# A state-space layer's front on Trainium2: B and x products in column halves around the context product, and TensorE's order tied per chunk

## The chip, the cores and the metric

The kernel runs on one core of a Trainium2 chip. The core has a matrix engine (TensorE, in the profile PE, its weight loads PEld), a vector engine (VectorE, DVE), an activation engine (ScalarE, ACT), a third elementwise engine (GpSimd, POOL) and a queue that issues transfers (SyncE, SP). Each engine takes its instructions in a fixed order and waits at an instruction until that one's inputs and outputs are free. Matrix products land in PSUM, which has eight banks of 512 fp32 columns for 128 partitions.

The metric is the device time of the whole program in microseconds, as the median of several runs.

## The reference

Two layers work on a latent stream of 1024 positions and a context of 256, both 1024 wide. Layer 0 is windowed attention, and the change does not touch it. Layer 1 is a bidirectional Mamba-2 (SSD) mixer. What matters of it:

```
z, xbc, dt_raw = split(h @ w_in)                       # for latent and context
xbc = silu(centred_depthwise_conv(xbc, conv_w, conv_b))  # 5 taps, zero padding
xs, bm, cm = split(xbc)                # 8 groups of 4 heads of 64; B and C of 128 per group
dt = softplus(dt_raw + dt_bias)        # two directions
# context: only its final states s_f and s_b are wanted
# latent, each direction, in chunks of 128 positions, starting from s_f or s_b:
states = einsum(bm, decay_to_end, xs * dt)             # per chunk
h_prev = scan of the states over the chunks
y_diag = einsum(cm @ bm.T, lmat, xs * dt)              # inside a chunk
y_off  = einsum(cm, h_prev, exp(a_cs))                 # from earlier chunks
u = (y_f + y_b + d_skip * xs) * silu(z)
out = (rms_normalize per group (u) * norm_w) @ w_out
```

Then a gated residual and a final normalisation follow.

## The kernel before

Every product of layer 1's front is made of three matmuls per tile of 128 rows: operands are split into a high and a low part (wh, wl for weights, uH, uL for the stream), and high x high, low x high and high x low are summed in PSUM. The stream lies transposed, as two latent tiles of 512 columns and one context tile of 256.

**The group's front** (`front`, line 1022 on). The layer works by the 8 groups. The front of a group makes four convolved tiles of 128 channels, in the order B (`bT`), the two halves of x (`cacc`, called x0 and x1 here) and C (`cT`), and then z. For B, x0 and x1 (`nat` in the code) there is also the context's product. In the program's order a tile is: context product (24 matmuls of 256 columns, line 1085, into the one-bank tile `psD`), then the latent product (48 matmuls of 512 columns, line 1095, into the two-bank tile `raw` of slot `pj2`; each pair works on columns 0 to 511 and 512 to 1023). Only the first tile of the first group makes its latent product in two halves, with the dt product (line 1105) between them. z is 2 x 2 x 4 x 12 matmuls of 256 columns (line 1129), again into `pj2`.

**After a product** come the taps (`taps`): ScalarE scales the middle tap into `acc` (line 1007) and VectorE adds four shifted ones (line 1011), all reading `raw`; then `silu`: a tanh on ScalarE that writes over `raw` (line 1018) and a product on VectorE (line 1019). B and x are also needed with positions on the partitions, so `natural` turns them: TensorE transposes `acc` back into `raw` (line 1058) and ScalarE copies the result out (line 1061). For the latent tiles this is done in two steps of four transposes and one copy each. The weights of the next tile are split by ScalarE (line 1034) and VectorE (line 1038).

**Who issues when.** `front` is a generator that yields after each matmul, with its cost (`N512`, `N256`). What follows a product is put on a queue, `post`: per 0.5 us of yielded cost one step is issued, credit that is not used is kept, and steps marked `LATE` (turnings and what depends on them) are issued 3 us of cost later. 

**The scan** runs beside it. In the main loop (line 1340 on) `slot` handles one chunk of group g while `fill` runs a share of the front of group g+1 (75.65 us of cost by the program's rates, so 9.46 per chunk; in the last group it is the output product, line 1527). A slot opens with `pcb` = B.T C (line 1247), then the products with the carried states (lines 1249 and 1250, tile `po`), the next state (line 1256) and four products with the decay matrix M (line 1281); VectorE multiplies M by `pcb` (line 1251) and scales `po` (line 1260). At the next slot the finished rows are transposed (line 1312) and stored. Between the fills `tick` advances `states`, the backward chain of group g+1: GpSimd weights x (line 1173) and decays the state (line 1178), TensorE multiplies into `psD` (line 1198), and VectorE adds (line 1210), eleven times, one after the other.

**What sets the order.** The listing above is the program's order. When the program is built, a planner with its own model of time goes through it and may put an instruction of an engine ahead of an earlier one that it takes to be waiting, where no dependence forbids it. Buffers of a name are used in rotation: `pj2` has 2, `psX` (all tiles of a slot) 3, `psD` 1, which is all eight banks. `tc.issue_after(x)` holds the instructions of a block that run on x's engine behind x in that engine's order; it adds no wait.

Of the kernel before, what the change touches and what calls it, by code (L numbers as in the profile page):

```python
# [9 lines left out]
F32 = mybir.dt.float32  # L10
# [7 lines left out]
P = 128  # L18
D = 1024
KT = D // P  # L20
LAT = 1024
CTX = 256
# [20 lines left out]
    pj=1, S=2, pt=2, pv=1,  # L43
# [18 lines left out]
LATE = 3.0  # L62
# [49 lines left out]
class Kernel:  # L112
# [908 lines left out]
    def front(self, g, st, post, first=None, dt=None):  # L1021

        nc, t, a = self.nc, self.t, self.a
# [27 lines left out]
            return lambda: weights(a["w_z"][g, q], 4, 256)  # L1051

        def natural(raw, acc, dst, o, n):
            steps = []

            def tr(lo, hi):
                for x in range(lo, hi):
                    nc.tensor.transpose(raw[:, x * P : (x + 1) * P], acc[:, x * P : (x + 1) * P], self.ident)

            def ev(d, lo, hi):  # L1060
                nc.scalar.copy(d[:, :, o : o + P], raw[:, lo * P : hi * P].rearrange("p (c n) -> p c n", n=P))  # L1061
# [14 lines left out]
        for n, (x, kind) in enumerate(tiles):  # L1076
            need(w)
            cur, w = w, (weights(a["w_dt"], KT, P) if g + n == 0 else loads[n + 1]())
            nat = {"bT": ("bn", 0), 0: ("xn", 0), 1: ("xn", P)}.get(kind)
            wh, wl = cur["h"], cur["l"]  # L1080
            if nat:
                raw = t(ps, [P, 512], F32, "psD")[:, :CTX]
                for k in range(KT):
                    for y, (l, r) in enumerate(((wh, uH), (wh, uL), (wl, uH))):
                        nc.tensor.matmul(raw, l[:, k, :], r[2][:, k, :], start=k + y == 0, stop=k == KT - 1 and y == 2)  # L1085
                        yield N256
                acc = t(pf, [P, CTX], F32, "cctx")
                post.extend(self.taps(x, raw, acc, 0, CTX, CTX) + self.silu(raw, acc) + natural(raw, acc, [(st[nat[0]][2], 0, 2)], nat[1], 2))
            raw = t(ps, [P, LAT], F32, "pj2")
            acc = t(pf, [P, LAT], F32, "cacc") if nat and kind != "bT" else t(p, [P, LAT], F32, kind)  # L1090
            for q in ((0,), (1,)) if g == 0 and n == 0 else ((0, 1),):
                for k in range(KT):
                    for y, (l, r) in enumerate(((wh, uH), (wh, uL), (wl, uH))):
                        for i in q:
                            nc.tensor.matmul(raw[:, 512 * i : 512 * i + 512], l[:, k, :], r[i][:, k, :], start=k + y == 0, stop=k == KT - 1 and y == 2)  # L1095
                            yield N512
                    if k == 3 and (q[0] == 0 or g + n == 0):
                        post.extend(w["steps"])
                if g + n == 0 and q[0] == 0:
                    need(w)  # L1100
                    dw, w = w, loads[1]()
                    draw = t(ps, [P, 512], F32, "psX")
                    for k in range(KT):
                        for y, (l, r) in enumerate(((dw["h"], uH), (dw["h"], uL), (dw["l"], uH))):
                            nc.tensor.matmul(draw, l[:, k, :], r[1][:, k, :], start=k + y == 0, stop=k == KT - 1 and y == 2)
# [13 lines left out]
        for i in range(2):  # L1119
            pj = t(ps, [P, 4, 256], F32, "pj2")  # L1120
            for q in range(2):
                ww = (w0, w)[q]
                need(ww)
                for c in range(4):
                    for k in range(4):
                        u, v = uH[i][:, 4 * q + k, c * P : (c + 1) * P], uL[i][:, 4 * q + k, c * P : (c + 1) * P]
                        for y, (l, r) in enumerate(((u, ww["h"]), (u, ww["l"]), (v, ww["h"]))):

                            nc.tensor.matmul(pj[:, c], l, r[:, k, :], start=c % 2 + q + k + y == 0, stop=c % 2 == 1 and q == 1 and k == 3 and y == 2)  # L1129
# [12 lines left out]

            post.extend([tanh, prod])

    def ssd(self, c0):
# [92 lines left out]
        def slot(n, st, fill, tick):  # L1238
# [8 lines left out]
            nc.tensor.matmul(pcb, st["bT"][:, cs], st["cT"][:, cs], start=True, stop=True)  # L1247
            po = t(ps, [P, 512], F32, "psX")
            nc.tensor.matmul(po[:, :256], st["cT"][:, cs], flat(st["hf"]), start=True, stop=True)  # L1249
            nc.tensor.matmul(po[:, 256:], st["cT"][:, cs], flat(st["hb"][c]), start=True, stop=True)  # L1250
# [95 lines left out]
        with ExitStack():  # L1346
            for g in range(G):
# [41 lines left out]
    def ssd_out(self, p, spare, sp, sc, post):  # L1389
# [107 lines left out]
        for n, (i, mg, qs) in enumerate(sweeps):  # L1497
# [8 lines left out]
            for q in qs:  # L1506
# [5 lines left out]
                for z in range(2):  # L1512
# [11 lines left out]
                    for x in range(4):  # L1524
                        sl = slice(x * P, (x + 1) * P)
                        for y, (l, r) in enumerate(((w["h"], hi), (w["h"], lo), (w["l"], hi))):
                            nc.tensor.matmul(banks[x], l[:, z, sl], r, start=k == 2 * qs[0] and y == 0, stop=k == 2 * qs[-1] + 1 and y == 2)  # L1527
# [166 lines left out]
```

## Time and profile before

| | |
|---|---|
| time, median of 3 runs | 1811.74 us (1805.05 to 1812.2) |
| the profiled execution's own time | 1807.02 us |
| its span, first to last instruction | 1805.3 us |
| mean granted TensorE clock | 0.993 |
| first front of the SSD layer | about 747 to 849 us |
| seven groups, front of the next beside the scan | about 849 to 1591 us |
| last group's scan beside the output product | about 1591 to 1694 us |
| rest of the output product | to 1805 us |

How to read the rows that follow. A row of the page's first part has an engine's busy time, its share of the span and the number of instructions. A row of groups has the line, the engine, the operation and its tiles (written by the names of the program, buffer numbers left out; the slot `pj2` appears as pj), shapes and count, then busy time, the mean of one in ns, and after the second bar the idle time of the engine just before these instructions with what ended it. A row of a timeline has start, duration, engine, line, operation and count, and in brackets the idle time before it with its releaser. TensorE's durations overlap, since matmuls are pipelined: what a matmul costs is the distance from its start to the next one's. A row of stretches has the length, then busy time and count for PE, PEld, DVE, ACT and POOL, the granted clock, the DMA share and GB/s. A row of waits has who waited for whom, the total, how often, and the longest.

### The profile page before, as it was taken

What the parts mean: (1) busy time and instruction counts of PE and PEld (TensorE: products, weight loads), DVE (VectorE), ACT (ScalarE), POOL (GpSimd) and SP (SyncE); (2) the same over time, 40 slices, a digit from 0 to 9 for tenths busy, and PEclk for the clock granted to TensorE, in tenths of its full rate; (3) what the DMA queues carried; (4) which work ended last, traced back from release to release, by engine and by line L of the source; (5) the groups of instructions that cost most, each with busy time, mean ns of one, the idle gap of its engine ahead of it and who ended that gap; (6) DMA issues with size and microseconds to landing.
All of it is one profiled execution on the core that took longest, in us unless ns stands there. A gap on an engine that the chain in (4) does not pass through costs nothing.

```text
span 1805.3 us, 28983 instructions
## 1 busy us (share of the span) xinstructions
PE 1739.6 (96%) x10319; PEld 1494.7 (83%) x10319; DVE 1181.8 (65%) x2115; ACT 867.1 (48%) x1906; POOL 799.0 (44%) x1068
## 2 busy tenths in 40 slices
PE   6899999999999999999999999999999999999997
PEld 2697788888888887778888898988889898888887
DVE  4634436778877885684776858577684867766734
ACT  3612237777777774452443525344353534544522
POOL 2331127555575545103454544645454464554411
PEclk9999999999999999999999999999999999999999
DMA  9558856444455436222222323222332322656533
GB/s 334 226 144 268 283 177 149 106 100 111 111 153 130 120 102 221 73 53 73 71 77 82 92 62 98 79 71 79 81 93 62 100 73 76 174 169 170 175 101 121
DMA packets 212495, 227.61 MB, mean 126 GB/s; under 512 B 16384, under 2 KB 149632, under 8 KB 212352
## 3 DMA queue, kind: packets, MB, share of 16 engines
q1 hardware_dynamic: 178288, 207.12, 38.0%
q0 software_dynamic: 34064, 18.65, 5.8%
q8 instruction: 81, 1.33, 0.3%
q14 instruction: 62, 0.51, 0.1%
HBM read 190.88 MB, written 35.13 MB: 125 GB/s over the span
## 4 chain that ended last, share of the span: by engine, by line
PE 81%; DVE 9%; ACT 4%; DMA 3%; issue 2%; SPq 1%; POOL 1%; DVEq 0%; ACTq 0%; POOLq 0%
PE pj L1095 17%; PE pj L1129 10%; PE pj L1527 7%; PE pj L246 6%; PE pj L247 6%; PE pj L248 6%; PE psD L1085 4%; PE psX L1281 3%; PE pt L684 3%; PE psD L1198 2%; PE pv L691 2%; PE pv L690 1%; PE S L659 1%; PE S L658 1%; PE psX L1249 1%
## 5 line engine op out<-in xcount | busy, mean ns | idle before, releaser
L246 PE MATMUL pj<-uH,wh 128*128 128x512 f32 (+1 forms) x712 | 257.4, 363 | 9.0 <-ACT uH L470 6.3
L247 PE MATMUL pj<-uL,wh 128*128 128x512 f32 (+1 forms) x712 | 243.3, 342 | 0.5 <-POOL uL L707 0.4
L248 PE MATMUL pj<-uH,wl 128*128 128x512 f32 (+1 forms) x712 | 242.4, 341 | 1.4 <-POOL wl L231 1.4
L1095 PE MATMUL pj<-uH,wl 128*128 128x512 f32 x512 | 172.7, 405 | 0.0
L1095 PE MATMUL pj<-uH,wh 128*128 128x512 f32 x512 | 171.4, 405 | 1.2 <-ACT bn L1061 0.7
L1095 PE MATMUL pj<-uL,wh 128*128 128x512 f32 x512 | 169.2, 402 | 0.0
L246 PEld LDWEIGHTS pj<-uH,wh 128*128 128x128 f32 x712 | 135.6, 191 | 36.2 <-ACT uH L470 7.7
L1129 PE MATMUL pj<-wh,uH 128*128 128x256 f32 x512 | 150.3, 294 | 9.1 <-ACT xn L1061 9.1
L1173 POOL TENSOR_TENSOR xw<-xn,dtdec 128x256 f32<-128x256 f32 x144 | 92.9, 650 | 141.6 <-PE psD L1198 107.1
L1129 PE MATMUL pj<-wh,uL 128*128 128x256 f32 x512 | 152.7, 298 | 0.0
L248 PEld LDWEIGHTS pj<-uH,wl 128*128 128x128 f32 x712 | 135.0, 190 | 18.6 <-POOL wl L231 2.3
L247 PEld LDWEIGHTS pj<-uL,wh 128*128 128x128 f32 x712 | 135.8, 191 | 16.0 <-issue 3.0
L1129 PE MATMUL pj<-wl,uH 128*128 128x256 f32 x512 | 146.7, 287 | 0.0
L689 DVE TENSOR_TENSOR pl<-pt,ph 128x512 fp32r<-128x512 f32 x168 | 114.1, 688 | 47.2 <-ACT ph L688 46.2
L231 POOL TENSOR_TENSOR wl<-wr,wh 128x512 fp32r<-128x512 f32 x76 | 100.2, 1322 | 86.1 <-ACT wh L229 85.2
L663 DVE CUSTOM_DVE_ANT_0 sm<-S,mask,nsink 128x640 f32<-128x640 f32 (+2 forms) x160 | 119.2, 773 | 19.8 <-PE S L659 12.6
L665 ACT ACTIVATE sm<-sm,nm 128x640 f32<-128x640 f32 (+2 forms) x160 | 118.6, 742 | 16.6 <-DVE nm L663 15.9
L688 ACT CAST ph<-pt 128x512 fp32r<-128x512 f32 x168 | 97.5, 586 | 56.0 <-PE pt L684 52.7
L229 ACT CAST wh<-wr 128x512 fp32r<-128x512 f32 (+1 forms) x116 | 74.7, 648 | 87.7 <-PE pj L247 63.5
L1095 PEld LDWEIGHTS pj<-uH,wl 128*128 128x128 f32 x512 | 95.3, 188 | 19.2
L1095 PEld LDWEIGHTS pj<-uL,wh 128*128 128x128 f32 x512 | 95.4, 188 | 18.7
L1129 PEld LDWEIGHTS pj<-wh,uH 128*128 128x128 f32 x512 | 98.7, 193 | 13.5 <-ACT xn L1061 12.1
(339 smaller groups left out, 4810.8 us busy)
## 6 DMA issues: line engine op xcount, KB each, us to landing
wr<-w_x SPq DMA_DIRECT2D x32, 512.0 KB, 4.6
M<-acs SPq DMA_DIRECT2D x64, 256.0 KB, 4.9
bw<-acs SPq DMA_DIRECT2D x64, 256.0 KB, 5.5
wr<-w_sk SPq DMA_DIRECT2D x24, 512.0 KB, 3.8
wr<-wg SPq DMA_DIRECT2D x40, 256.0 KB, 4.5
qs<-q POOLq DMA_DIRECT2D x40, 256.0 KB, 3.9
wada<-w_ada SPq DMA_DIRECT2D x16, 512.0 KB, 7.2
wr<-wq SPq DMA_DIRECT2D x32, 256.0 KB, 3.0
```

The source lines that it names most:

```text
L231: (eng or nc.vector).tensor_tensor(l, raw, h, op=ALU.subtract)
L246: self.nc.tensor.matmul(ps, lh, rh, start=first and i == 0, stop=False)
L247: self.nc.tensor.matmul(ps, lh, rl, start=False, stop=False)
L248: self.last_mm = self.nc.tensor.matmul(ps, ll, rh, start=False, stop=last and i == n - 1)
L663: nc.vector.tensor_tensor_reduce(out=sm[:, :W], in0=Sv, in1=self.mask[:, m0 : m0 + W], scale=-SCALE, scalar=self.nsink[:, 4 * j + r : 4 * ...
L665: nc.scalar.activation(sm[:, :W], sm[:, :W], AF.Exp, bias=nm[:, r : r + 1], scale=-1.0, accum_out=sums[:, r : r + 1])
L688: nc.scalar.copy(ph, ptf)
L689: nc.vector.tensor_sub(pl, ptf, ph)
L1095: nc.tensor.matmul(raw[:, 512 * i : 512 * i + 512], l[:, k, :], r[i][:, k, :], start=k + y == 0, stop=k == KT - 1 and y == 2)
L1129: nc.tensor.matmul(pj[:, c], l, r[:, k, :], start=c % 2 + q + k + y == 0, stop=c % 2 == 1 and q == 1 and k == 3 and y == 2)
L1173: nc.gpsimd.tensor_tensor(xw, X(st, c).rearrange("p (r h) -> p r h", r=R), self.dtdec[:, c, hd(d, g)].unsqueeze(2).broadcast_to([P, R, HP] ...
L1527: nc.tensor.matmul(banks[x], l[:, z, sl], r, start=k == 2 * qs[0] and y == 0, stop=k == 2 * qs[-1] + 1 and y == 2)
```

## The change

Four edits, nothing else:

1. B, x0 and x1 are made in column halves in every group: columns 0 to 511, then the context product, then columns 512 to 1023. (The first tile of the first group keeps context product, first half, dt product, second half.) The context product is now a generator of its own, `ctx`.
2. The taps of columns 0 to 509 are posted at the end of the first half, and with them the split of the next weights; the taps of columns 510 to 1023 after the second half. The tanh and the product of `silu` stay whole.
3. A turning issues all its transposes (8 for a latent tile) and then its copies.
4. `pcb` is held behind the last filling matmul issued before it, and what a fill issues on TensorE (its matmuls, and the transposes that `post` issues then) behind the `pcb` of its chunk.

```diff
         def natural(raw, acc, dst, o, n):
-            steps = []
-
-            def tr(lo, hi):
-                for x in range(lo, hi):
+
+            def tr():
+                for x in range(n):
                     nc.tensor.transpose(raw[:, x * P : (x + 1) * P], acc[:, x * P : (x + 1) * P], self.ident)
...
-            for d, lo, hi in dst:
-                steps.append(lambda lo=lo, hi=hi: tr(lo, hi))
-                steps.append(lambda d=d, lo=lo, hi=hi: ev(d, lo, hi))
-            return [(LATE, steps)]
+            return [(LATE, [tr] + [lambda d=d, lo=lo, hi=hi: ev(d, lo, hi) for d, lo, hi in dst])]
...
-            if nat:
-                raw = t(ps, [P, 512], F32, "psD")[:, :CTX]
+            def ctx():
+                cr = t(ps, [P, 512], F32, "psD")[:, :CTX]
                 for k in range(KT):
                     for y, (l, r) in enumerate(((wh, uH), (wh, uL), (wl, uH))):
-                        nc.tensor.matmul(raw, l[:, k, :], r[2][:, k, :], start=k + y == 0, stop=k == KT - 1 and y == 2)
+                        self.pe = nc.tensor.matmul(cr, l[:, k, :], r[2][:, k, :], start=k + y == 0, stop=k == KT - 1 and y == 2)
                         yield N256
                 acc = t(pf, [P, CTX], F32, "cctx")
-                post.extend(self.taps(x, raw, acc, 0, CTX, CTX) + self.silu(raw, acc) + natural(raw, acc, [(st[nat[0]][2], 0, 2)], nat[1], 2))
+                post.extend(self.taps(x, cr, acc, 0, CTX, CTX) + self.silu(cr, acc) + natural(cr, acc, [(st[nat[0]][2], 0, 2)], nat[1], 2))
+
+            if nat and g + n == 0:
+                yield from ctx()
...
-            for q in ((0,), (1,)) if g == 0 and n == 0 else ((0, 1),):
+            for q in ((0,), (1,)) if nat else ((0, 1),):
+                if q[0] == 1 and g + n > 0:
+                    yield from ctx()
                 for k in range(KT):
...
-                            nc.tensor.matmul(raw[:, 512 * i : 512 * i + 512], ...)
+                            self.pe = nc.tensor.matmul(raw[:, 512 * i : 512 * i + 512], ...)
                             yield N512
-                    if k == 3 and (q[0] == 0 or g + n == 0):
+                    if k == 3 and (q[0] == 0 and not nat or g + n == 0):
                         post.extend(w["steps"])
+                if nat and q[0] == 0:
+                    post.extend(self.taps(x, raw, acc, 0, 510, LAT) + (w['steps'] if g + n else []))
...
-            post.extend(self.taps(x, raw, acc, 0, LAT, LAT) + self.silu(raw, acc))
+            if nat:
+                post.extend(self.taps(x, raw, acc, 510, LAT, LAT) + self.silu(raw, acc))
+            else:
+                post.extend(self.taps(x, raw, acc, 0, LAT, LAT) + self.silu(raw, acc))
...
-            nc.tensor.matmul(pcb, st["bT"][:, cs], st["cT"][:, cs], start=True, stop=True)
+            with self.tc.issue_after(self.pe.ins):
+                self.opened = nc.tensor.matmul(pcb, st["bT"][:, cs], st["cT"][:, cs], start=True, stop=True)
...
                     while spent < until:
-                        cost = next(work, None)
-                        if cost is None:
-                            return
-                        spent += cost
-                        post.run(cost)
+                        with self.tc.issue_after(self.opened.ins):
+                            cost = next(work, None)
+                            if cost is None:
+                                return
+                            spent += cost
+                            post.run(cost)
```

The matmuls of z and of the output product also set `self.pe`.

More of the change, by code (lines that the diff above doesn't have):

```diff
@@ L1094, in front @@
                         for i in q:
-                            nc.tensor.matmul(raw[:, 512 * i : 512 * i + 512], l[:, k, :], r[i][:, k, :], start=k + y == 0, stop=k == KT - 1 and y == 2)
+                            self.pe = nc.tensor.matmul(raw[:, 512 * i : 512 * i + 512], l[:, k, :], r[i][:, k, :], start=k + y == 0, stop=k == KT - 1 and y == 2)
                             yield N512
-                    if k == 3 and (q[0] == 0 or g + n == 0):
+                    if k == 3 and (q[0] == 0 and not nat or g + n == 0):
                         post.extend(w["steps"])
+                if nat and q[0] == 0:
+                    post.extend(self.taps(x, raw, acc, 0, 510, LAT) + (w['steps'] if g + n else []))
                 if g + n == 0 and q[0] == 0:
@@ L1127, in front @@
                         for y, (l, r) in enumerate(((u, ww["h"]), (u, ww["l"]), (v, ww["h"]))):
-                            nc.tensor.matmul(pj[:, c], l, r[:, k, :], start=c % 2 + q + k + y == 0, stop=c % 2 == 1 and q == 1 and k == 3 and y == 2)
+                            self.pe = nc.tensor.matmul(pj[:, c], l, r[:, k, :], start=c % 2 + q + k + y == 0, stop=c % 2 == 1 and q == 1 and k == 3 and y == 2)
                             yield N256
@@ L1526, in ssd_out @@
                         for y, (l, r) in enumerate(((w["h"], hi), (w["h"], lo), (w["l"], hi))):
-                            nc.tensor.matmul(banks[x], l[:, z, sl], r, start=k == 2 * qs[0] and y == 0, stop=k == 2 * qs[-1] + 1 and y == 2)
+                            self.pe = nc.tensor.matmul(banks[x], l[:, z, sl], r, start=k == 2 * qs[0] and y == 0, stop=k == 2 * qs[-1] + 1 and y == 2)
                             yield N512
```

## The prediction

> **What bounds the kernel now.** I read the page first, then the waits of TensorE between 849 and 1591 us, then the stretches, then one steady group instruction by instruction.
>
> ```profile
> PE 1739.6 (96%) x10319; PEld 1494.7 (83%) x10319; DVE 1181.8 (65%) x2115; ACT 867.1 (48%) x1906; POOL 799.0 (44%) x1068
> PE 81%; DVE 9%; ACT 4%; DMA 3%; issue 2%; SPq 1%; POOL 1%; DVEq 0%; ACTq 0%; POOLq 0%
> ```
> ```profile
> 849.00:955.00 106.00, 104.69 (x655) 94.03 (x655) 73.59 (x124) 44.66 (x104) 53.63 (x76) 1.00 0.30 78
> ...
> 1485.00:1591.00 106.00, 104.69 (x652) 93.81 (x651) 79.31 (x132) 48.98 (x114) 55.02 (x73) 1.00 0.45 133
> 747.00:849.00 102.00, 94.52 (x543) 82.04 (x544) 68.45 (x91) 44.76 (x87) 12.32 (x20) 0.97 0.21 50
> ```
> ```profile
> PE pj L1129 <- ACT xn L1061: 9.1, 7, 1.3
> ```
>
> The change touches the seven steady groups (849 to 1591, about 106 us each), the first front (747 to 849), and through the ties the last group. In a steady group TensorE is busy 104.69 of 106 us. All its waiting there is one wait, once per group: the z product waits 1.3 us for the eviction of the second x tile, 9.1 us in all. So the gain is capped: 9.1 us here and part of the 7.5 us (102 less 94.52) in the first front. A loss has no such cap: every wait put into TensorE's queue is paid seven or eight times.
>
> VectorE is the second engine, and its share of the group misleads, because the stage that the change touches is the crowded one:
>
> ```profile
> 1061.00:1074.60 13.60, 13.60 (x67) 11.43 (x65) 4.50 (x9) 1.75 (x3) 4.63 (x7) 1.00 0.19 54
> 1074.60:1092.20 17.60, 17.60 (x101) 15.24 (x100) 15.12 (x25) 8.69 (x20) 7.28 (x10) 1.00 0.20 61
> 1092.20:1111.60 19.40, 19.40 (x116) 16.78 (x114) 16.02 (x29) 10.07 (x27) 10.01 (x14) 1.00 0.35 95
> 1111.60:1127.00 15.40, 15.40 (x91) 13.55 (x90) 13.78 (x24) 9.23 (x21) 5.74 (x7) 1.00 0.43 118
> ```
>
> In the third column of numbers after the length VectorE is busy 15.12 of 17.60, 16.02 of 19.40 and 13.78 of 15.40 us while the three tiles are convolved, 83 to 89%. Today TensorE never waits for that, because a tile's taps run under the next product.
>
> **The change, part by part.**
>
> *Halves and early taps.* For each of bT, x0, x1 the order becomes: columns 0 to 511 (24 matmuls), the context product (24), columns 512 to 1023 (24). TensorE's own time does not change, since the same instructions run in another order:
>
> ```profile
> 747.86 3.13 PE psD L1085 x24
> 750.99 5.47 PE pj L1095 x24
> ...
> 863.70 2.87 PE psD L1085 x24
> ```
>
> A half already takes 5.47 us for 24 (0.228 each); the context product takes 2.87.
>
> Each tap becomes two instructions:
>
> ```profile
> L1011 DVE SCALAR_TENSOR_TENSOR cacc<-pj,cw,cacc 128x1022 f32<-128x1022 f32 (+1 forms) x64 | 81.7, 1277 | 0.8
> ...
> L1011 DVE SCALAR_TENSOR_TENSOR cctx<-psD,cw,cctx 128x254 f32<-128x254 f32 (+1 forms) x96 | 45.8, 477 | 0.6
> ...
> L1007 ACT ACTIVATE cctx<-psD,cb,cw 128x256 f32<-128x256 f32 x24 | 13.4, 560 | 0.0
> ```
> ```profile
> 1092.73 1.20 ACT L1007 ACTIVATE cacc<-pj,cb,cw 128x1024 f32<-128x1024 f32 x1
> ```
>
> A line through 254 columns at 477 ns and 1022 at 1277 gives 744 ns for 510; two of them cost 211 ns more than one whole tap. Four taps in three tiles: 2.5 us of VectorE per group. ScalarE's first tap by its two rows is 0.77 us for half, 0.35 more for both, 1.0 us per group. Both lie beside TensorE's work, so I cost them at nothing directly; without cover the 2.5 us would be paid in the crowded stage.
>
> The split of the next tile's weights moves from the middle of the product to the end of the first half, behind the early taps:
>
> ```profile
> L1038 DVE TENSOR_TENSOR wl<-wr,wh 128x1024 fp32r<-128x1024 f32 x49 | 59.9, 1223 | 15.1 <-ACT wh L1034 13.9 <-PE psX L964 1.2
> L1034 ACT CAST wh<-wr 128x1024 fp32r<-128x1024 f32 x49 | 51.1, 1043 | 52.3 <-PE psD L1085 41.3 <-PE pj L1129 5.6 <-PE psX L1105 3.0
> ```
>
> Its 1.04 and 1.22 us have the context product and the second half, 2.87 and 5.47 us, to hide under: nothing; its load keeps its place on SP's queue. Without that cover the next tile would start 2.3 us late.
>
> *The wait that this brings.* The second half's matmuls write the bank next to the one that the early taps read, in one two-bank tile (raw, slot pj2). The early taps stand ahead of them in program order: the post queue gets some 72 steps per group at 0.5 us against 75.65 us of work (192 matmuls at 0.229 and 264 at 0.120, the program's own rates, as the rows above have them), so its credit piles up, and a posted step is issued at the next matmul. Whether the matmuls must wait depends on whether such accesses are ordered by bank or by tile. The trace has the case: the four transposes into the second bank of a tile, behind the eviction that reads the first.
>
> ```profile
> 781.90 0.66 PE L1058 MATMUL pj<-ident,bT 128*128 128x128 f32 x4 [0.52 <-DVE bT L1019]
> 783.64 0.66 PE L1058 MATMUL pj<-ident,bT 128*128 128x128 f32 x4 [1.09 <-ACT bn L1061]
> ```
> ```profile
> 783.02 0.57 ACT L1061 COPY bn<-pj 128x512 f32<-128x512 f32 x1
> ```
>
> The eviction of columns 0 to 511 ends at 783.59; the transposes into columns 512 on start at 783.64, after 1.09 us of waiting for it. So a write to one bank waits for a read of the other. I carry this to the second half: its first matmul waits for the fourth early tap.
>
> The Trainium skill, "PSUM — Partial Sum Buffer", section "PSUM bank collisions raise a hardware error", says that only accesses of the same bank and partition quadrant collide, and that different banks run clean; it asks for a guard by bank. By that rule the second half need not wait and the sum below would lose its three positive terms. The trace disagrees as far as this kernel's guards go (1.09 us).
>
> How late is the fourth early tap? Today's whole taps after the end of x0 and x1:
>
> ```profile
> 1094.72 2.60 DVE L1011 SCALAR_TENSOR_TENSOR cacc<-pj,cw,cacc 128x1022 f32<-128x1022 f32 x2
> ...
> 1099.71 1.27 DVE L1011 SCALAR_TENSOR_TENSOR cacc<-pj,cw,cacc 128x1022 f32<-128x1022 f32 x1
> ...
> 1121.12 1.27 DVE L1011 SCALAR_TENSOR_TENSOR cacc<-pj,cw,cacc 128x1022 f32<-128x1022 f32 x1
> ```
> ```profile
> 1112.94 1.20 ACT L1007 ACTIVATE cacc<-pj,cb,cw 128x1024 f32<-128x1024 f32 x1 [0.20 <-PE pj L1095]
> ```
>
> x0: from 1092.73 to 1100.98, 8.25 us for 6.3 us of work (1.20 and four of 1.277). x1: 1112.94 to 1122.39, 9.45 us. Other instructions in VectorE's queue add 1.9 to 3.1 us. For halves the bare chain is 0.77 + 4 x 0.744 = 3.75 us; the additions scaled by 3.75/6.3 are 1.1 to 1.9; so 4.9 to 5.6 us. Cover: the context product, 2.87, and the scan's own matmuls, which take 30 of a group's 106 us beside 75.65 us of filling, 1.1 in that time: 4.0. Left: 0.9 to 1.6. I take **1.3 us each for x0 and x1**. Bounds: 0, where the scan's matmuls collect there; 4.0, where none do and VectorE's whole 3.1 stays (3.75 + 3.1 - 2.87). Behind the waiting matmul stand in TensorE's queue the rest of the tile and, by the tie, the next chunk's opening matmul, for which VectorE's product L1251 waits.
>
> bT meets the group's start:
>
> ```profile
> 1061.00 0.80 PE L1095 MATMUL pj<-uH,wh 128*128 128x512 f32 x2
> ...
> 1069.62 0.59 PE L1198 MATMUL psD<-xw,bn 128*128 128x256 f32 x2
> 1070.05 0.59 PE L1256 MATMUL psX<-xw,bn 128*128 128x256 f32 x2
> 1070.48 1.00 PE L1281 MATMUL psX<-xn,M 128*128 128x64 f32 x8
> ...
> 1074.35 0.59 PE L1250 MATMUL psX<-hb,cT 128*128 128x256 f32 x2
> 1074.59 0.47 PE L1085 MATMUL psD<-uH,wh 128*128 128x256 f32 x1
> ...
> 1078.21 0.38 PE L1247 MATMUL psX<-cT,bT 128*128 128x128 f32 x2
> ```
> ```profile
> 1070.33 0.42 DVE L1210 TENSOR_TENSOR hb<-hb,psD 128x256 f32<-128x256 f32 x1 [5.04 <-PE psD L1198]
> ...
> 1074.98 0.69 DVE L1260 TENSOR_TENSOR y<-psX,eacs 128x512 f32<-128x512 f32 x1 [3.87 <-PE psX L1250]
> ```
>
> The one psD buffer belongs to the state chain until 1070.75. So in the build before the whole bT main product runs first (1061.00 to 1074.35) and the context product after it. With halves, 24 matmuls (5.47) and the scan's pieces (two L1198 and one L1256 at 0.43 from start to start, L1281 about 0.8: 2.1) last until about 1068.6. Then the context product waits for psD, at most until 1070.75, and the second half for taps that end near 1067 + 0.3 + 3.75 = 1071; the context product that covers them ends at 1071.5 to 1073.6. I take **1.0 us** (0 to 2.2).
>
> *Turnings in one step.* Eight transposes, then two evictions, where the second four waited for the first eviction. In the steady groups TensorE fills that pause today, so it saves latency only, and that meets the z wait:
>
> ```profile
> 1129.64 0.60 PE L1058 MATMUL pj<-ident,cacc 128*128 128x128 f32 x4
> 1132.82 0.60 PE L1058 MATMUL pj<-ident,cacc 128*128 128x128 f32 x4
> 1136.13 0.39 PE L1129 MATMUL pj<-wh,uH 128*128 128x256 f32 x1 [1.30 <-ACT xn L1061]
> ```
>
> The two sets are 3.2 us apart, more than the wait of 1.30. Against it: x1's context product no longer runs after x1, so the way from its end to the z product is 2.87 us shorter; for it: only 4 x 0.744 of taps remain, 2.1 less. I take **-1.0 us** (-1.3 to 0).
>
> *Ties.* The opening matmul of chunk c (L1247) comes after all filling of chunk c-1, and the filling of chunk c after it. Today chunk 1 opens at 1078.21, behind 48 + 24 + 2 filling matmuls, 14.3 us by their rates; its position in the program is after 9.46. Its psX buffer is the one that L1260 releases (three buffers, five tiles a chunk), so it waits for the same state chain. Up to 4.8 us of filling that now bridges the chain would stand behind it. But L1250 ran at 1074.35 by its place in the queue, 3.6 us after its input (1070.75), so without work ahead of it the release would come near 1071.9, about when the bT halves resume. I take 0 beyond bT's 1.0, bounds 0 and 4.8.
>
> *First front.* bT's second half is covered by the dt product (24 of 512 columns). x0 and x1 wait behind the dt chain on VectorE:
>
> ```profile
> 776.62 4.14 DVE L980 RECIPROCAL sz<-sz 128x640 f32<-128x640 f32 x1
> ```
>
> With that in its queue, I take 2 us each, 4 in all (0 to 9).
>
> *Sum.* Per group 1.0 + 1.3 + 1.3 - 1.0 = 2.6, times 7 is 18; with the first front 22. The profiled execution took 1807.02 us (span 1805.3 and 1.7 around it), 4.7 below the median of 1811.74 and inside its runs. 1807.0 + 22 = **1829 us**.
>
> **Rivals.**
>
> (a) *The ordering does not bite, and the kernel gets faster*, either because second halves are ordered by bank or because the context and scan matmuls cover the taps wholly. Decided by the fourth early tap ending within about 4.0 us of the first half's end. Then the z wait goes (-9.1) and a few us in the first front: 1807 - 9 - 4 = 1794. For it: the bare chain is 3.75. Against: the row at 783.64, and VectorE at 83 to 89%. Chance 0.2.
>
> (b) *It cancels*: waits of about 1 us per group against the z wait, 1807 to 1816. Also the case that the planner of the order moves the halves together again, so that the change does little. Chance 0.17.
>
> (c) *The ties stall the group's start too*, because the chain's last matmuls are no earlier: 4.8 us x 8 groups on top, with 1.0 for bT then contained in it: 1829 + 8 x 3.8 = 1859. For it: 14.3 against 9.46. Against: hb was ready 3.6 us before it was used. Chance 0.18.
>
> My forecast, waits of 1 to 5 us per group net, has 0.45; its own range is 1818 to 1842.
>
> **Numbers.** About 0.5% (9 us) is what a measurement of this kernel can tell from no change. Faster by more: (a), 0.2. Within: (b) and the low edge of the forecast, 0.18. Slower: the rest, 0.62. The range runs from (a) to just over (c): 1794 to 1862.
>
> **What would show it.** Right: TensorE's waits in the steady groups show L1095 released by DVE L1011, some three per group of 1 to 2 us, VectorE's share over 73.6 per 106 us, and groups of 108 to 109 us. The z wait gone or under 0.5 us shows the turning step right. (a) is shown by no row of L1095 behind L1011; (c) by L1247 or L1095 waiting near the group's start for L1260 or L1210, 4 us or more. The forecast is wrong if VectorE's early taps end while the context product runs, or if the period of a group falls under 105.8 us.

## The result and the profile after

| | us | against the kernel before |
|---|---|---|
| kernel before, median of 4 runs | 1808.78 | |
| changed kernel, median of 4 runs (1854.86 to 1860.24) | 1858.34 | 1.0273, 95% interval 1.0255 to 1.0291 |
| profiled execution of the changed kernel | 1854.86, span 1853.2 | |

The change costs 49.6 us; 22 were forecast. The page's first block (busy time, share of the span, instructions) and its line of shares of the chain of waits, after:

```profile
PE 1753.3 (95%) x10319; PEld 1505.4 (81%) x10319; DVE 1196.8 (65%) x2211; ACT 876.2 (47%) x1928; POOL 789.3 (43%) x1068
PE 74%; DVE 14%; ACT 3%; issue 3%; DMA 3%; POOL 1%; SPq 1%; DVEq 0%; POOLq 0%; ACTq 0%
```

VectorE's share of the chain rose from 9 to 14%. TensorE has the same 10,319 matmuls, yet is busy 13.7 us longer (1739.6 before). So there are two things to find: new waits, and matmuls that became slower.

The stretches, one row for each of the seven steady groups, then the first front, then the seven groups together. After the length come busy us of TensorE, its weight loads, VectorE, ScalarE and GpSimd, then the granted clock:

```profile
860.40:969.50 109.10, 106.12 (x659) 95.08 (x657) 75.85 (x139) 47.15 (x108) 52.56 (x77) 1.00 0.29 77
969.50:1080.00 110.50, 105.05 (x654) 94.19 (x652) 74.76 (x136) 46.80 (x109) 52.04 (x75) 1.00 0.29 77
1080.00:1195.00 115.00, 108.23 (x653) 96.42 (x651) 75.10 (x136) 46.65 (x109) 52.56 (x75) 0.97 0.27 70
1195.00:1310.00 115.00, 108.22 (x648) 96.22 (x646) 73.62 (x133) 45.85 (x108) 52.29 (x74) 0.96 0.28 73
1310.00:1418.50 108.50, 105.89 (x657) 94.75 (x655) 75.80 (x139) 47.28 (x110) 51.84 (x75) 1.00 0.30 84
1418.50:1530.00 111.50, 105.84 (x649) 94.65 (x648) 74.61 (x133) 45.81 (x108) 51.91 (x74) 0.98 0.28 71
1530.00:1636.80 106.80, 104.17 (x648) 93.17 (x647) 80.05 (x142) 49.71 (x116) 50.62 (x71) 1.00 0.43 132
746.00:860.40 114.40, 95.99 (x547) 83.59 (x548) 72.33 (x105) 42.45 (x87) 14.60 (x22) 0.94 0.17 45
...
860.40:1636.80 776.40, 743.53 (x4551) 664.49 (x4550) 529.78 (x952) 329.24 (x762) 363.84 (x517) 0.99 0.31 83
```

The same stretch of the seven groups in the kernel before, from the first matmul L1247 to the first of the last product, L1527:

```profile
849.30:1589.50 740.20, 731.05 (x4553) 655.31 (x4551) 516.44 (x869) 318.65 (x739) 372.76 (x517) 1.00 0.32 87
```

The seven groups grew by 36.2 us: TensorE's idle time from 9.2 to 32.9 (length less busy), its busy time by 12.5, for the same matmuls. The four groups at a clock of 1.00 last 109.1, 110.5, 108.5 and 106.8, mean 108.7, the forecast's 108 to 109. The other three, at 0.96 to 0.98, last 111.5 to 115. The front, from the first matmul of the first context product to the first opening matmul of a chunk, grew by 12.7 us (101.4 to 114.1); pieces ahead of it and behind the groups moved by under 2 us.

TensorE's waits in the seven groups (engine, line, what ended the wait: us in all, times, longest):

```profile
PE pj L1096 <- DVE cacc L1011: 16.3, 10, 3.3
PE pj L1096 <- DVE bT L1011: 11.8, 7, 2.4
PE pj L1096 <- ACT bn L1060: 4.2, 4, 1.1
PE pj L1135 <- ACT xn L1060: 0.3, 2, 0.2
```

28.1 us are second halves behind early taps: 17 waits in 21 tiles, from 0.2 to 3.3 us long. 4.2 us are four times 1.05 us in which x1's first half, started ahead of x0's second, waits for bT's buffer. z's wait (last row) fell from 9.1 to 0.3. One of the waits for taps, with the queues of TensorE, VectorE and ScalarE (start, length; in brackets the idle time before and what ended it):

```profile
1201.84 0.28 PE L1081 MATMUL psD<-uH,wh 128*128 128x256 f32 x1
...
1202.85 0.75 DVE L1011 SCALAR_TENSOR_TENSOR bT<-pj,cw,bT 128x508 f32<-128x508 f32 x1 [1.62 <-ACT bT L1007]
...
1204.50 0.72 DVE L1236 COPY_PREDICATED M<-before,bw 128x512 f32<-128x512 int32 x1
...
1206.50 0.74 DVE L1011 SCALAR_TENSOR_TENSOR bT<-pj,cw,bT 128x510 f32<-128x510 f32 x1
...
1207.38 0.47 PE L1096 MATMUL pj<-uH,wh 128*128 128x512 f32 x1 [2.42 <-DVE bT L1011]
...
1208.62 0.44 PE L1254 MATMUL psX<-cT,bT 128*128 128x128 f32 x2
1208.85 1.07 PE L1256 MATMUL psX<-hf,cT 128*128 128x256 f32 x2
1209.71 1.06 PE L1257 MATMUL psX<-hb,cT 128*128 128x256 f32 x2
```

The context product follows the first half at 1201.84; the four early taps end at 1207.24, 5.4 us later (4.9 to 5.6 were forecast), because the chunk's M and y steps stand between them on VectorE. Then the second half starts. What the forecast had no term for begins 1.5 us later: pairs L1256 and L1257 start 0.86 us apart, where such a pair took 0.43 before (1070.05 to 1070.48). The stretches on both sides of that instant:

```profile
1207.40:1208.80 1.40, 1.40 (x7) 1.18 (x8) 1.19 (x3) 0.61 (x2) 0.36 (x1) 1.00 0.81 55
1208.90:1212.20 3.30, 3.30 (x9) 2.66 (x9) 2.56 (x7) 0.18 (x1) 1.11 (x2) 0.50 0.19 25
```

The granted clock is 0.50 for about 3.4 us, and matmuls take twice as long in it: each such stretch costs 1.7 us on top of the wait. There are five such stretches in the seven groups, 20.5 us long in all (the last section has their starts). TensorE is busy for 19.4 us of them, so they cost 9.7 us. That is most of the 12.5 us of extra busy time. In the group rows it is what the clock column is short of 1.00.

The first front, its two long waits (8.36 and 6.13 us, in the brackets) with rows around them:

```profile
784.47 0.82 DVE L993 TENSOR_TENSOR xn<-xn,cacc 128x640 f32<-128x640 f32 x1
785.35 0.90 PE L964 MATMUL psX<-ident,xn 128*128 128x128 f32 x3 [8.36 <-DVE xn L993]
787.57 0.74 DVE L1011 SCALAR_TENSOR_TENSOR cacc<-pj,cw,cacc 128x510 f32<-128x510 f32 x1
788.37 0.76 PE L1096 MATMUL pj<-uH,wh 128*128 128x512 f32 x1
...
798.16 1.28 ACT L1242 ACTIVATE M<-M,vf 128x128 f32<-128x128 f32 x4 [7.87 <-DVE M L1236]
800.96 1.05 ACT L1060 COPY bn<-pj 128x512 f32<-128x512 f32 x2
802.06 0.80 PE L1096 MATMUL pj<-uH,wh 128*128 128x512 f32 x1 [6.13 <-ACT bn L1060]
```

x0's early taps share VectorE with the dt chain and the other taps. TensorE stands until the transposes of the dt chain (L964) can run; its second half starts at 788.37, where the last early tap ends (788.31). x1's first half then needs bT's buffer, whose eviction (L1060) stands on ScalarE behind M at 798.16.

### The profile page after: what moved, and what is told of

It is laid out like the page before. It is cut to its first block, busy times and chain, and to the rows that moved or that the text cites. A ratio compares the mean times of both kernels' runs of the same rounds, so it can differ in the third digit from the quotient of the medians.

```text
span 1853.2 us, 29147 instructions
## 1 busy us (share of the span) xinstructions
PE 1753.3 (95%) x10319; PEld 1505.4 (81%) x10319; DVE 1196.8 (65%) x2211; ACT 876.2 (47%) x1928; POOL 789.3 (43%) x1068
## 4 chain that ended last, share of the span: by engine, by line
PE 74%; DVE 14%; ACT 3%; issue 3%; DMA 3%; POOL 1%; SPq 1%; DVEq 0%; POOLq 0%; ACTq 0%
PE pj L1096 16%; PE pj L1135 10%; PE pj L1535 7%; PE pj L246 6%; PE pj L247 6%; PE pj L248 6%; PE pt L684 3%; PE psX L1288 2%; DVE cacc L1011 2%; PE pv L691 2%; PE psD L1204 2%; PE psX L1256 1%; PE pv L690 1%; PE psX L1257 1%; PE S L659 1%
## 5 line engine op out<-in xcount | busy, mean ns | idle before, releaser
L1096 PE MATMUL pj<-uH,wh 128*128 128x512 f32 x512 | 204.1, 418 | 39.8 <-DVE cacc L1011 16.3
L1096 PE MATMUL pj<-uH,wl 128*128 128x512 f32 x512 | 200.4, 409 | 1.1 <-DVE wl L1038 1.1
L1096 PE MATMUL pj<-uL,wh 128*128 128x512 f32 x512 | 196.1, 402 | 0.0
L246 PEld LDWEIGHTS pj<-uH,wh 128*128 128x128 f32 x712 | 135.6, 191 | 34.4 <-issue 6.3
L1179 POOL TENSOR_TENSOR xw<-xn,dtdec 128x256 f32<-128x256 f32 x144 | 91.9, 642 | 167.5 <-PE psD L1204 114.2
L1096 PEld LDWEIGHTS pj<-uH,wh 128*128 128x128 f32 x512 | 97.3, 191 | 63.8 <-ACT bn L1060 11.5
L689 DVE TENSOR_TENSOR pl<-pt,ph 128x512 fp32r<-128x512 f32 x168 | 114.2, 688 | 47.7 <-ACT ph L688 46.6
L663 DVE CUSTOM_DVE_ANT_0 sm<-S,mask,nsink 128x640 f32<-128x640 f32 (+2 forms) x160 | 119.2, 772 | 19.9 <-PE S L659 12.7
```

The source lines that it names most:

```text
L246: self.nc.tensor.matmul(ps, lh, rh, start=first and i == 0, stop=False)
L663: nc.vector.tensor_tensor_reduce(out=sm[:, :W], in0=Sv, in1=self.mask[:, m0 : m0 + W], scale=-SCALE, scalar=self.nsink[:, 4 * j + r : 4 * ...
L689: nc.vector.tensor_sub(pl, ptf, ph)
L1096: self.pe = nc.tensor.matmul(raw[:, 512 * i : 512 * i + 512], l[:, k, :], r[i][:, k, :], start=k + y == 0, stop=k == KT - 1 and y == 2)
L1179: nc.gpsimd.tensor_tensor(xw, X(st, c).rearrange("p (r h) -> p r h", r=R), self.dtdec[:, c, hd(d, g)].unsqueeze(2).broadcast_to([P, R, HP] ...
```

## The experiments

**e1 to e3: the turning alone, the ties alone, all but the ties.**

e1, the kernel before with

```diff
...
-            for d, lo, hi in dst:
-                steps.append(lambda lo=lo, hi=hi: tr(lo, hi))
-                steps.append(lambda d=d, lo=lo, hi=hi: ev(d, lo, hi))
-            return [(LATE, steps)]
+            return [(LATE, [tr] + [lambda d=d, lo=lo, hi=hi: ev(d, lo, hi) for d, lo, hi in dst])]
```

> Before plus the turning in one step alone. Theory (the second half's wait for the early taps makes the loss): the turning only saves latency; the z wait of 1.3 us a group shrinks or goes, so 1798 to 1809 us against 1809 before. Rival (the ties make the loss): says the same here.

1828.94 us, ratio 1.0112 (1.0091 to 1.0133): a miss in the time, though what the theory says of z holds. Its wait is nearly gone, 0.6 us in the seven groups where the kernel before has 9.1:

```profile
PE pj L1125 <- ACT xn L1060: 0.6, 1, 0.6
```

The groups take 737.7 us, 2.5 less, but the last group's stage (first to last matmul of the last product) grew from 154.5 to 173.0. The longest of its waits, where the kernel before has none:

```profile
PE psD L1194 <- DVE hb L1206: 2.6, 1, 2.6
```

The state chain is later there. Groups and last stage together take 16 us more than before: TensorE waits 17.4 us in place of 9.1, and spends 13.7 us at a granted clock of 0.50 (none before), of which it is busy 12.2, so they cost 6. Why the turning alone makes the state chain late stays open; the changed kernel, which has the same turning, does not show it (154.5).

e2, the kernel before with

```diff
+            with self.tc.issue_after(self.pe.ins):
+                self.opened = nc.tensor.matmul(pcb, ...)
...
+                        with self.tc.issue_after(self.opened.ins):
                             cost = next(work, None)
```

> Before plus the ties alone. Theory: without halves the ties hold back little, 1804 to 1815 us. Rival (the ties take the filling that bridged the state chain at each group's start, up to 4.8 us a group): 1825 us or more, with TensorE waiting near the group's start.

1858.55 us, ratio 1.0267 (1.0241 to 1.0292), groups 790.5: in the rival's range, but not where the rival saw it. Only 5.4 us of the waits are behind the state chain. Tied, TensorE can no longer fill the pause between the two turning steps:

```profile
PE pj L1058 <- ACT bn L1061: 10.5, 6, 1.8
PE pj L1129 <- ACT xn L1061: 9.5, 5, 3.2
PE pj L1058 <- ACT xn L1061: 8.1, 6, 2.2
```

All waits of the groups are 36.3 us here, 27 more than before. TensorE's busy time rose by 23 us (731.0 to 754.1) at a granted clock of 0.97 over the groups: the slow stretches cost not much less than the waits.

e3, the changed kernel without its ties (edit 4):

> After without the ties. Theory: the early taps' wait stays, 1848 to 1865 us, with L1096 still released by DVE L1011 in the steady groups. Rival (ties): 1835 us or less.

1851.36 us, ratio 1.0234 (1.0216 to 1.0252), groups 768.0, front 114.2, as the theory expected. So in the changed kernel, whose turning is one step, the ties cost 8.4 us of the groups, not 50. The waits for the taps stay without them:

```profile
PE pj L1096 <- DVE cacc L1011: 17.3, 7, 2.7
```

**e4 and e5: without the early taps, without the halves.**

e4, the changed kernel with

```diff
-                    post.extend(self.taps(x, raw, acc, 0, 510, LAT) + (w['steps'] if g + n else []))
+                    post.extend(w['steps'] if g + n else [])
...
-                post.extend(self.taps(x, raw, acc, 510, LAT, LAT) + self.silu(raw, acc))
+                post.extend(self.taps(x, raw, acc, 0, LAT, LAT) + self.silu(raw, acc))
```

> After with whole taps posted behind the second half; halves, ties and turning stay. Theory: the second half no longer waits, so no L1096 behind DVE L1011, the granted clock stays at 1.0 in the steady groups, 1798 to 1818 us. Rival (ties, or the place of the context product): 1835 us or more.

1821.12 us, ratio 1.0072 (1.0047 to 1.0098), 3 us over the expected range. Front 103.2, groups 751.4. The early taps cost 37 of the 49.6 us: 10.9 in the front and 25.0 in the groups. Without them z's wait is back, larger than before (9.1), and two of these waits have a stretch of 3.4 us at a granted clock of 0.50 behind them, where the theory expected none:

```profile
PE pj L1135 <- ACT xn L1060: 14.8, 7, 2.2
```

e5, the kernel before with turning and ties, without halves (edits of e1 and e2 together):

> The kernel before with the turning in one step and with TensorE's order tied, but with whole tiles: the change without its halves and early taps. Theory (the halves and early taps carry most of the loss, and what the ties cost alone came from the two-step turning, whose transposes waited for evictions 10.5 + 8.1 us in the seven groups): 1805 to 1825 us, seven groups of 735 to 755 us, the waits of the transposes for ScalarE's evictions gone. Rival (the ties cost their 50 us by themselves, whatever the turning): 1845 to 1865 us, seven groups of 780 us or more.

1842.31 us, ratio 1.0171 (1.0149 to 1.0193), groups 770.9: between the two expectations. The transposes' waits for evictions are gone, as the theory had it, but the context product now waits:

```profile
PE psD L1081 <- ACT xn L1060: 15.3, 7, 2.5
PE psD L1057 <- DVE cctx L1019: 6.5, 1, 6.5
```

So the halves by themselves (e5 to e4) gain 21 us, and the early taps (e4 to the changed kernel) lose 37. From the kernel before to the changed one this makes 32 for turning and ties (e5), less 21, plus 37: 48 of the 49.6 us.

**e6: one-bank tiles.** The two banks of each product tile become two tiles, also for z and the last product, so a second half writes a tile that no early tap reads. Taps that cross the boundary, tanh, its product and z's steps are split to match. The main lines:

```diff
-            raw = t(ps, [P, LAT], F32, "pj2")
+            raw = [t(ps, [P, 512], F32, "pj2") for _ in range(2)]
...
-   self.pe = nc.tensor.matmul(raw[:, 512 * i : 512 * i + 512], l[:, k, :], ...)
+   self.pe = nc.tensor.matmul(raw[i], l[:, k, :], ...)
...
```

> The changed kernel with the two banks of a product tile as two separate one-bank tiles (also for z and the last product), so that nothing orders the second half's matmuls behind the early taps; each whole tap that crosses the boundary becomes two, and tanh, its product and z's two steps become halves. Theory (the order by tile makes the wait, and the wait with the low clock behind it makes most of the loss): the products' waits for VectorE's taps, 28.1 us in the seven groups, vanish, no stretch of half clock behind them, front 102 to 108 us, groups 735 to 755 us, 1800 to 1825 us. Rival (the wait is only the sign that VectorE is too slow for the halves, and would come back as a wait of the next tile's transposes or slots): 1835 us or more, with waits of 20 us or more in the groups on VectorE or on the slots.

1798.03 us, ratio 0.9933 (0.9912 to 0.9953): 60 us under the changed kernel, 12 under the one before and 2 under the theory's range, though VectorE has 144 instructions more than in the changed kernel. The stretches of the seven groups and of the front:

```profile
847.10:1576.70 729.60, 729.02 (x4558) 657.39 (x4557) 557.43 (x1080) 337.23 (x809) 375.76 (x522) 1.00 0.33 88
...
748.40:847.10 98.70, 92.39 (x544) 81.09 (x545) 72.64 (x121) 45.87 (x95) 11.96 (x19) 0.98 0.21 52
```
TensorE is busy 729.02 of 729.60 us in the groups. The overlap that the order by tile forbade is seen directly (taps are L1015 here, the product L1122):

```profile
1066.50 3.10 DVE L1015 SCALAR_TENSOR_TENSOR bT<-pj,cw,bT 128x510 f32<-128x510 f32 x4
...
1067.92 0.40 PE L1122 MATMUL pj<-uH,wh 128*128 128x512 f32 x1
```

Four early taps read the first half until 1069.60, and the second half's matmuls run from 1067.92 on, without a wait. The rival, that VectorE is the bound and the wait would come back elsewhere, is refuted.

**e7: the idle time filled.** The changed kernel, with matmuls whose sums are overwritten, ahead of each context product:

```diff
+                if g:
+                    for k in range(12):
+                        nc.tensor.matmul(cr, wh[:, k % KT, :], uH[2][:, k % KT, :], start=k == 0, stop=k == 11)
```

> The changed kernel with 12 extra matmuls of the context product ahead of each context product in the seven steady groups (their sums are overwritten by the real ones): about 12 x 0.12 = 1.44 us more work for TensorE per tile, 30 us in 21 tiles, in the place where it idles. Theory (part of the loss is the granted clock, which falls to 0.50 for 3.4 us behind an idle time of 2.4 us or more): the waits for the early taps shrink by about the extra work where they were longer than it, the half clock of 20.4 us in the groups is gone or nearly (10 us saved), and the time ends between 1850 and 1864 us although 30 us of work were added. Rival (the clock falls for another reason, or costs nothing): half clock stays at 14 us or more in the groups and the time is 1866 us or more, since of the 30 us only some 15 us fit into the waits.

1846.23 us, ratio 1.0195 (1.0174 to 1.0215): 12 us faster than the changed kernel with 30 us more for TensorE to do, and 4 us better than the theory's range. The seven groups, and their only wait:

```profile
868.80:1630.80 762.00, 758.87 (x4807) 688.44 (x4805) 535.78 (x954) 329.85 (x760) 361.45 (x517) 1.00 0.32 85
```
```profile
PE pj L1099 <- DVE bT L1011: 3.1, 6, 0.5
```

The granted clock is 1.00 throughout. Less the 252 extra matmuls at 0.12 (30.2), TensorE is busy 728.6 us, 14.9 less than in the changed kernel for the same matmuls, and close to e6's 729.02. So the extra busy time of the changed kernel goes when its idle times are filled.

**e8 to e11: what of the change is worth having on one-bank tiles.** e8 puts e4's edit on e6 (late taps), e9 leaves the ties out of e6, e10 is e5 with one-bank tiles, e11 is the kernel before with one-bank tiles alone.

> The kernel of one-bank tiles with the first half's taps put back behind the second half (halves around the context product, turning and ties stay). Theory (early taps are worth having once nothing is ordered behind them: they end each tile's chain earlier, which takes away z's wait for the second x tile's eviction): that wait comes back, 1.3 to 2.2 us per group (9 to 15 us in all), front 100 to 104 us, groups 739 to 752 us, 1807 to 1821 us. Rival (one-bank tiles alone are the gain, because a tile's banks come free one by one; the early taps add nothing): 1794 to 1803 us, no wait of z over 0.5 us per group.

1797.84 us, ratio 0.9934 (0.9912 to 0.9956), groups 729.6, with 0.6 us of waiting in them and none of z: the rival's case. On one-bank tiles the early taps bring nothing; whole taps behind the second half do as well. e4 and e8 differ in their tiles alone, by 23 us. So of the 60 us between the changed kernel and e6, 37 are what the early taps cost there (e4), and 23 come from one-bank tiles without any early tap.

> The kernel of one-bank tiles without the ties of TensorE's order. Theory (the ties only move where TensorE waits; where no product waits for taps there is little to move): 1793 to 1804 us, groups 725 to 737 us. Rival (in the changed kernel the ties cost 8.4 us in the groups, 776.4 against 768.0 us without them, and cost the same here): 1787 to 1792 us, groups 719 to 723 us. Other rival (the ties are what keeps the products from running ahead of the chunk work, as the output product's row shows in the changed kernel without them, psX waiting 4.7 us for VectorE's y): 1805 us or more, with waits of the chunk work's matmuls on DVE y of 5 us or more.

1809.25 us, ratio 1.0005 (0.999 to 1.0019). The groups take 730.1 us as the theory expected, but the last group's stage takes 169.0 us against 152.6 in e6; no expectation had that. The time is in the range of the other rival (1805 us or more), but the waits on VectorE's y that it names are not there. The state chain makes TensorE wait there, as in e1:

```profile
PE psD L1232 <- DVE hb L1244: 3.4, 2, 2.7
```

The waits of that stage add up to 5.6 us, and one stretch of 3.4 us at a granted clock of 0.50 costs 1.7; the rest is not resolved. The ties are worth about 11 us here.

> One-bank tiles with the turning in one step and the ties, without halves: the kernel of e5 with one-bank tiles. Theory (the halves are worth having with one-bank tiles too, since in two-bank tiles they took 1842 to 1821 us: the first half's bank is written before the context product, so a tile's transposes and slots are asked for later): waits of 1 to 2.5 us per group on ScalarE's evictions stay, groups 738 to 755 us, 1806 to 1825 us. Rival (with one-bank tiles a slot comes free bank by bank, which removes the same waits that the halves removed, so the halves add nothing): groups 728 to 734 us, 1794 to 1803 us.

1827.44 us, ratio 1.0091 (1.0055 to 1.0127), groups 765.5: above the theory's range for both, so further from the rival. z waits again, and the context product with it:

```profile
PE pj L1151 <- ACT xn L1086: 16.9, 7, 2.4
PE psD L1107 <- ACT xn L1086: 5.5, 7, 3.0
```

Six stretches of 3.4 us at a granted clock of 0.50 in the groups add some 10 us. The halves are worth 30 us on one-bank tiles (e10 to e8).

> The kernel before with one-bank tiles and nothing of the change. Theory (the order by tile is what z waits for in the kernel before: it takes the whole two-bank tile once the second x tile's last eviction is through): z's wait of 1.3 us per group goes, 9 us in all, 1797 to 1804 us, groups 729 to 735 us. Rival (the wait is for the bank itself, or returns elsewhere): 1807 to 1815 us, groups 737 to 742 us.

1821.33 us, ratio 1.0066 (1.0043 to 1.0089). The time is above both ranges. z's wait is gone, as the theory had it, but small waits for other releasers, 10.3 us in all, take its place, as the rival had it, and the groups stay at 741.1 us. The largest of them:

```profile
PE pj L1121 <- DVE wl L1062: 3.1, 10, 0.5
```

The last group's stage is 167.5 us; like that of e1 and e9 it is long without the ties, though that of the kernel before and of e3, which have none either, is not. What decides there stays open. The best kernels of the study, e6 and e8, have halves, turning, ties and one-bank tiles together. Without the ties (e9), the halves (e10) or the one-bank tiles (e4) the time is 11, 30 or 23 us longer; no run leaves out the turning alone.

## Why the prediction was right and wrong

**Right: the mechanism.** Second halves wait for the fourth early tap because the order goes by tile. e6 shows it: the same matmuls and taps in separate tiles have none of the 28.1 us. The sum of these waits held too: 28.1 / 7 = 4.0 us per group, where the terms were 1.0 + 1.3 + 1.3 = 3.6. In part that is luck: bT has 1.7, not 1.0, x0 and x1 together 2.3, not 2.6, and single waits spread from 0.2 to 3.3 us where 1 to 2 were expected. The spread matters, because only the long ones have a slow stretch behind them.

**Right: z's wait.** -8.8 / 7 = -1.3 per group, where -1.0 was taken. The working gave two causes, the turning and the shorter tail of taps, and a loss against them, the earlier end of x1's context product. The runs fit all three: the turning alone takes the wait from 9.1 to 0.6 us (e1); with the halves, but without the early taps, it is 14.8, 2.1 per group (e4); the early taps bring it down to 0.3.

**Right: VectorE's and ScalarE's extra work at nothing**, as far as e6 shows: with still more instructions on VectorE, TensorE waits 0.6 us in seven groups.

**Wrong: the sum, where it counts a wait as its length.** The step that failed is that TensorE's own time does not change, since the same instructions run in another order: in the groups it rose by 12.5 us. The sum had no term for the granted clock, though the profile's rows of before give one for each stretch. Five of the waits of 1.9 us and more are followed by 3.4 or 6.8 us at 0.50; that is 9.7 us in the groups, and e7 shows that it goes when the idle time is filled. The Trainium skill, "TensorE: Matmul & The Clock Gate", section "Part 1: The HAM clock gate (the "warmup" mystery)", says that TensorE gets half its clock after an idle window of some 3.4 us; the traces agree in the length and the depth of the stretch, but see the last section on the idle time.

**Wrong: the first front**, 4 us forecast, 12.7 measured. The range of 0 to 9 named the right place, VectorE's dt chain, but it let x0 wait about 2 us; TensorE stood 8.4. And it left out the buffers: x1's first half needs bT's tile, whose eviction had become late on ScalarE, 6.1 us. The clock fell here as well (0.94 against 0.97), but mostly inside the waits: TensorE is busy for 7.6 us at 0.50 where the kernel before has 6.2, so it cost under 1 us more.

**Small: buffers in the groups and the ties.** Waits for bT's buffer (4.2 us) had no term. The ties were taken at 0 with a bound of 4.8 per group; e3 gives 8.4 / 7 = 1.2. That they cost so little hangs on the other parts: with whole tiles, ties and turning cost 32 us (e5).

Together, in the groups: 28.1 + 4.2 - 8.8 + 9.7 = 33.2 of the 36.2 us. With 12.7 in the front that is 45.9 of the 47.9 by which the span grew. Against the forecast's 22 the clock in the groups (9.7) and the front (8.7 more than its 4) are the two large terms.

**The rivals.** (a), that the ordering doesn't bite, is what e6 builds: 1798, where 1794 was worked out. (c), the ties stalling each group's start, gave 1859, nearly the measured time, for a reason that the trace refutes: in the seven groups no row has the chunk's opening matmul waiting, and without ties (e3) the time is still 1851. That the prediction's widest range, to 1862, takes in the measured 1858 is owed to this rival, so it is luck.

## What to carry to other kernels

Before work is split so that a part can be read while the rest is written, see whether the program orders accesses by tile; if so, split the tile as well (1858 to 1798 us here). Price an idle time of TensorE of some 1.8 us or more as its length plus 1.7 us for a slow stretch that may follow, as the next section shows. And undo a bundle part by part: here the halves gain 21 to 30 us, the ties cost 49 or 7 or gain 11 depending on what stands beside them, and the early taps lose 37 or nothing.

## What the runs showed of the hardware

The granted clock falls after shorter idle times than the 3.4 us of the Trainium skill's page "TensorE: Matmul & The Clock Gate", and not after all of them. Two waits of the changed kernel:

```profile
1022.40 0.47 PE L1096 MATMUL pj<-uH,wh 128*128 128x512 f32 x1 [2.45 <-DVE cacc L1011]
...
1430.54 0.64 PE L1096 MATMUL pj<-uH,wh 128*128 128x512 f32 x1 [1.96 <-DVE bT L1011]
```

After the longer one the clock stayed at 1.00; after the shorter one it was 0.50. In the kernel before, seven waits of 1.30 to 1.31 us had no such stretch. What decides is where a wait lies. In the trace the five slow stretches of the seven groups start at 1092.76, 1137.13, 1208.81, 1249.77 and 1430.68 us, which is 13, 34, 46 and 99 times 3.413 us after the first. So in this trace the clock changes at the borders of a fixed raster of pieces of 3.413 us. The pieces around the two waits, with TensorE's busy time first and its clock third from the end:

```profile
1017.67:1021.08 3.41, 2.29 (x20) 2.08 (x18) 3.28 (x6) 1.95 (x5) 0.00 (x0) 1.00 0.62 218
1021.08:1024.49 3.41, 2.08 (x10) 1.79 (x11) 3.38 (x7) 0.54 (x1) 0.00 (x0) 1.00 0.00 0
1024.49:1027.90 3.41, 3.41 (x20) 2.91 (x20) 2.58 (x8) 0.39 (x1) 1.07 (x2) 1.00 0.00 0
...
1427.27:1430.68 3.41, 1.45 (x12) 1.27 (x11) 3.34 (x6) 2.82 (x9) 0.55 (x1) 1.00 0.33 91
1430.68:1434.09 3.41, 3.41 (x10) 2.74 (x11) 2.29 (x6) 0.39 (x1) 0.00 (x0) 0.50 0.23 52
```

The wait of 2.45 us is divided between two pieces, in which TensorE idles 1.12 and 1.33 us. The wait of 1.96 us lies in one piece, and the next piece runs at 0.50. The same count over the seven groups of all thirteen kernels, each with the raster of its own trace, for pieces that run at 1.00 themselves: all 30 with 1.93 us or more of idle time have a piece at 0.50 behind them, none of the 2816 with 1.76 us or less has, and of the 7 in between 4 have. So here the clock falls when TensorE idles for somewhat more than half of a piece (1.76 / 3.413 = 0.52, 1.93 / 3.413 = 0.57). Of the eight waits of 1.95 us and more in the groups of the changed kernel, five idle a piece for that long; the other three are divided by a border so that no piece has more than 1.44 us. Filling each gap with 1.44 us of matmuls was enough to keep 1.00 (e7), where no piece of the groups idles for more than 0.6 us.
